# The layout of the gate matrices in scratch: by token block, or by groups of four i1

## The chip, the cores and the metric

The kernel runs on one core of a Trainium2 chip. The metric is the device time of one execution in microseconds (us): from the start of the program on the core to its end, as a median over runs. A profiled execution is one more, recorded by the hardware profiler; its span runs from the first to the last instruction.

A core has TensorE (PE, matrix products; its weight loads are listed as PEld), VectorE (DVE), ScalarE (ACT), GpSimd (POOL) and SyncE (SP). Sixteen DMA engines move data between HBM and on-chip memory, in packets. Here SyncE issues all plain transfers, in the order of the program, into one queue (q1 in the profile), and GpSimd issues the indirect gathers into another (q0).

## What is computed

The reference is one layer of a decoder trunk for 1024 prompt tokens and 8 sample tokens: three branches (a dilated window attention, a convolution, an attention into memory) that are gated, summed and projected onto x, and then a mixer of very many single-neuron experts. Only the mixer matters here:

```python
def peer(x, w_pq, sub_keys, u_tab, v_tab):
    ...
        e = (jnp.take_along_axis(i1, ci // PEER_TOPK, axis=-1) * N_KEYS
             + jnp.take_along_axis(i2, ci % PEER_TOPK, axis=-1))
        g = jax.nn.softmax(sc, axis=-1)
    ...
        a = jnp.einsum('bd,bed->be', xb, u_tab[e], preferred_element_type=jnp.float32)
        hg = g * jax.nn.gelu(a)
        out = jnp.einsum('be,bed->bd', hg, v_tab[e].astype(jnp.float32))
```

There are 128 x 128 experts, numbered by a pair (i1, i2). Each token picks 128 of them (8 heads, 16 each), with a gate weight for each.

## The kernel before

The tokens are split. For the last three blocks of 128 prompt tokens, and for the samples, `peer_gather` fetches the picked rows of u and v one slot at a time: one indirect DMA on GpSimd's queue brings 128 rows of 8 KB (tile `uv`), VectorE makes the dot product (L985), ScalarE the gelu (L990), VectorE adds into `gacc` (L995). For the first five blocks (640 tokens) `peer_dense` computes every expert and multiplies by a gate that is zero for the experts not picked.

Those gates are built in `gate_build`, 32 tokens at a time (TC = 32): TensorE multiplies one-hot matrices (L1061, L1062), and ScalarE copies the result into `stg` (L1063), which holds i2 in its 128 partitions and, in each partition, i1 by 32 tokens, 16 KB in all. One DMA stores it to the scratch tensor `gscr` in HBM (L1066). There are 640 / 32 = 20 such stores of 2 MB. `stg` has two buffers. The first 16 stores are issued while the second half of the front (projections, gates, attention units) runs, the last four while the last top-k and the start of the dense part run.

`peer_dense` walks over the 128 values of i1 in groups of six (C = 6). For each i1 it loads the rows of u (`ur`, L1097), splits them into a high and a low part, makes the products with 640 tokens (`pa`), the gelu (L1107, tile `ge`) and the product with the gates (L1109). The gates come from tiles `Gt` with two buffers, each for four values of i1 (GC = 4) and loaded by one DMA (L1094): 32 loads of 1.25 MB. After the six i1 of a group come, for each half of the columns, six loads of v (`vr`, three buffers, L1121), their split (`vh` on ScalarE, L158; `vl` on VectorE, L159), the products `pv` into five banks of PSUM, and the sums into `dacc` on VectorE (L1129).

The order of the instructions on every engine, and of the DMAs that SyncE issues, is fixed when the program is built: a scheduler places them by the priorities in the code. The gather's instructions are placed between those of the dense part on VectorE, ScalarE and GpSimd, and no engine leaves its order at run time. A DMA waits, on SyncE, until the buffer that it writes is free, and all later DMAs wait with it.

Of the kernel before, what the change touches and what calls it, by code (L numbers as in the profile page):

```python
# [9 lines left out]
F32 = mybir.dt.float32  # L10
# [11 lines left out]
P = 128  # L22
# [7 lines left out]
NA = NAB * P  # L30
# [4 lines left out]
BIG = 3e38  # L35
GSCALE = 16384.0
TC = 32
LNPOS = (16, 12)
MIDPOS = (24, 20)
LATEPOS = (24, 22)  # L40
# [6 lines left out]
def peer_trunk(tc, I, O):  # L47
    nc = tc.nc
# [10 lines left out]
    with contextlib.ExitStack() as es:  # L59
        const = es.enter_context(tc.tile_pool(name="const", bufs=1))  # L60
        dram = es.enter_context(tc.tile_pool(name="dram", bufs=1, space=DRAM))
# [74 lines left out]
        oscr = [dram.tile([SEQ, 520], F32, name=f"oscr{g}") for g in range(3)]  # L136
        x1scr = dram.tile([NTOK, D], F32, name="x1scr")
        h2scr = dram.tile([NTOK, D], F32, name="h2scr")
        gscr = dram.tile([NA // TC, P, P, TC], F32, name="gscr")
        mscr = dram.tile([SEQ, 512], F32, name="mscr")  # L140
        gtscr = dram.tile([24, P, HALF + NS], F32, name="gtscr")
        saccd = dram.tile([P, D], F32, name="saccd")
# [14 lines left out]
        def split_load(raw, hi, lo):  # L157
            nc.scalar.copy(hi, raw)  # L158
            nc.vector.tensor_tensor(lo, raw, hi.bitcast(F32), op=OP.subtract)  # L159
# [98 lines left out]
        def front(hf, keep, wp):  # L258
# [53 lines left out]
            with tc.tile_pool(name=f"mix{hf}", bufs=1) as mx, banks(f"mix{hf}"):  # L312
# [337 lines left out]
                order = [*range(8, 24), *range(8)]  # L650
                for q in range(LNPOS[hf]):
                    gate(order[q])
# [12 lines left out]
                bh, bl = conv_norm()  # L665
                for q in range(LNPOS[hf], MIDPOS[hf]):
                    gate(order[q])
# [348 lines left out]
        def gate_build(gb, pgs, toks, TB, prio0=None, prio_step=0):  # L1016

            step = 0
            for t0 in range(toks[0], toks[1], TC):
                bi = t0 // P  # L1020
                if t0 % P == 0:
                    pt = pgs.tile([P, 4, P], F32, tag="pG", bufs=2, name=f"igT{bi}")
                    for q in range(3):
                        nc.tensor.transpose(pt[:, q], igT[bi][:, q], ident)
                    nc.scalar.copy(igT[bi], pt[:, 0:3])
                    ig = gb.tile([P, 4, P, 2], F16, tag="ig", bufs=1, name=f"ig{bi}")

                    def twice(q):
                        return igT[bi][:, q].unsqueeze(2).to_broadcast([P, P, 2])

                    for q in range(2):
                        nc.vector.tensor_copy(ig[:, q], twice(q))
                    nc.vector.tensor_scalar(ig[:, 2], twice(2), GSCALE, None, op0=OP.mult)
                    nc.vector.scalar_tensor_tensor(
                        ig[:, 3], twice(2), GSCALE, ig[:, 2], op0=OP.mult, op1=OP.subtract
                    )
                stg = gb.tile([P, P, TC], F32, tag="stg", bufs=2, name=f"stg{t0}")
                for tb in range(0, TC, TB):
                    ts_ = slice(t0 % P + tb, t0 % P + tb + TB)
                    if prio0 is not None:  # L1040
                        tc.cur_priority = prio0 + step * prio_step
                        step += TB // 4
                    o1, o2, wh = (
                        gb.tile([P, TB, P // 2, 2], F16, tag=f"oh{q}", bufs=2, name=f"oh{q}_{t0}_{tb}") for q in range(3)
                    )
                    shape = [P, TB, P // 2, 2]
                    ioB = iotaT.rearrange("p (a e) -> p a e", e=2).unsqueeze(1).to_broadcast(shape)

                    def cols(q):
                        return ig[:, q, ts_].unsqueeze(2).to_broadcast(shape)  # L1050

                    nc.vector.tensor_tensor(o1, ioB, cols(0), op=OP.is_equal)
                    nc.vector.tensor_tensor(o2, ioB, cols(1), op=OP.is_equal)
                    nc.vector.tensor_tensor(wh, o1, cols(2), op=OP.mult)
                    wl = o1
                    nc.vector.tensor_tensor(wl, o1, cols(3), op=OP.mult)
                    for t4 in range(0, TB, 4):
                        pG = pgs.tile([P, 4, P], F32, tag="pG", bufs=2, name=f"pG{t0}_{tb + t4}")
                        for t in range(t4, t4 + 4):
                            a, h, l = (x[:, t].rearrange("p a e -> p (a e)") for x in (o2, wh, wl))  # L1060
                            nc.tensor.matmul(pG[:, t - t4], a, h, start=True, stop=False)  # L1061
                            nc.tensor.matmul(pG[:, t - t4], a, l, start=False, stop=True)  # L1062
                        nc.scalar.activation(  # L1063
                            stg[:, :, tb + t4 : tb + t4 + 4], pG.rearrange("p t i -> p i t"), AF.Copy, scale=1.0 / GSCALE
                        )
                nc.sync.dma_start(gscr[t0 // TC], stg)  # L1066

        def peer_dense():
            NB = NAB
            with (  # L1070
# [10 lines left out]
                for b in range(NB):  # L1081
                    nc.sync.dma_start(acc[:, b], x1scr[b * P : (b + 1) * P, :])
                C = 6
                GC = 4
                HN = NA // 2
                for c in range(-(-P // C)):
                    if c == 5:
                        sample_out(dq)
                    hgs = []
                    group = range(c * C, min(P, c * C + C))  # L1090
                    for i1 in group:
                        if i1 % GC == 0:
                            Gt = dq.tile([P, NA // TC, GC, TC], F32, tag="Gt", bufs=2, name=f"Gt{i1}")
                            nc.sync.dma_start(Gt, gscr[:, :, i1 : i1 + GC, :].rearrange("n p i t -> p n i t"))  # L1094
                        raw = dp.tile([P, KD * P], F32, tag="uraw", bufs=2, name=f"ur{i1}")
                        uh = dp.tile([P, KD * P], F32R, tag="uh", bufs=2, name=f"uh{i1}")
                        nc.sync.dma_start(raw, I["uT"][i1])  # L1097
                        ul = dp.tile([P, KD * P], F32R, tag="ul", bufs=2, name=f"ul{i1}")
                        split_load(raw, uh, ul)
                        ge = dh.tile([P, NA], F32, tag="ge", bufs=2, name=f"ge{i1}")  # L1100
                        for q in range(2):
                            cs = slice(q * HN, (q + 1) * HN)
                            pa = t_tile(f"pa{i1}{q}")
                            for k in range(KD):
                                ks = slice(k * P, (k + 1) * P)
                                mm3(pa[:, :HN], uh[:, ks], ul[:, ks], h2h[:, k, cs], h2l[:, k, cs], k == 0, k == KD - 1)
                            nc.scalar.activation(ge[:, cs], pa[:, :HN], AF.Gelu_apprx_tanh)  # L1107
                        g3 = ge.rearrange("p (n t) -> p n t", t=TC)
                        nc.vector.tensor_tensor(g3, g3, Gt[:, :, i1 % GC, :], op=OP.mult)  # L1109
                        hh = dh.tile([P, NA], F32R, tag="hh", bufs=C, name=f"hh{i1}")  # L1110
                        hl = dh.tile([P, NA], F32R, tag="hl", bufs=C, name=f"hl{i1}")
                        nc.scalar.copy(hh, ge)
                        nc.vector.tensor_tensor(hl, ge, hh.bitcast(F32), op=OP.subtract)
                        hgs.append((hh, hl))
                    for q in range(2):
                        qs = slice(q * 512, q * 512 + 512)
                        pv = [mm_tile(f"pv{c}{q}{tb}") for tb in range(NB)]
                        for j, i1 in enumerate(group):
                            raw = dq.tile([P, 512], F32, tag="vraw", bufs=3, name=f"vr{i1}{q}")
                            vh = dq.tile([P, 512], F32R, tag="vh", bufs=3, name=f"vh{i1}{q}")  # L1120
                            nc.sync.dma_start(raw, I["v_tab"][i1 * P : (i1 + 1) * P, qs])  # L1121
                            vl = dq.tile([P, 512], F32R, tag="vl", bufs=3, name=f"vl{i1}{q}")
                            split_load(raw, vh, vl)
                            hh, hl = hgs[j]
                            for tb in range(NB):
                                ts_ = slice(tb * P, (tb + 1) * P)
                                mm3(pv[tb], hh[:, ts_], hl[:, ts_], vh, vl, j == 0, j == len(group) - 1)
                        for tb in range(NB):
                            nc.vector.tensor_tensor(acc[:, tb, qs], acc[:, tb, qs], pv[tb], op=OP.add)  # L1129
                            if group[-1] == P - 1:  # L1130
                                nc.sync.dma_start(O["y"][tb * P : (tb + 1) * P, qs], acc[:, tb, qs])
# [35 lines left out]
        tc.cur_priority = base  # L1167
        phase["mm"] = 5
        peer_dense()


# [79 lines left out]
```

## Time and profile before

| | us |
|---|---|
| median of 3 runs | 3676.84 |
| lowest and highest of the 3 | 3676.28, 3680.1 |
| the profiled execution | 3687.05 |
| its span, first to last instruction | 3685.3 |

The profile was taken on one execution, and durations below are its own. Busy time of an engine is time in which it works on an instruction; a wait is idle time of an engine together with what ended it. The clock of TensorE is granted in steps: 1.0 is full speed, 0.5 half. The view of DMA packets counts the packets that began in a stretch, by queue, with the share of 16 engines' time that they took; a packet is one run of bytes, and very small ones carry the signals that a transfer has landed. The span starts at 0 us in all views.

### The profile page before, as it was taken

How to read it: one execution, taken by the hardware profiler on the slowest of the kernel's cores; microseconds unless marked ns; L12 is line 12 of the kernel's file. 1: busy time of each engine (PE TensorE's matmuls, PEld its weight loads, DVE VectorE, ACT ScalarE, POOL GpSimd, SP SyncE). 2: the span in 40 equal slices, each digit the busy share in tenths (PEclk: the TensorE clock that was granted, in tenths of full speed). 3: DMA queues.
4: the chain of work that ended last, by engine and by line, in shares of the span. 5: the costliest groups of instructions: out<-in, count | busy, mean ns of one | idle time of the engine just before them, and what ended most of it. 6: DMA issues, size and time to landing. Idle time of an engine off the chain costs nothing.

```text
span 3685.3 us, 55180 instructions
## 1 busy us (share of the span) xinstructions
PE 3371.1 (91%) x19969; PEld 2953.3 (80%) x19969; DVE 2904.0 (79%) x6280; ACT 1492.0 (40%) x3519; POOL 565.3 (15%) x398
## 2 busy tenths in 40 slices
PE   8987999898888899787699999899998989899999
PEld 6766988697666778577699888899897979798988
DVE  4358554499999668789988888789887878797987
ACT  5553552235765465344433333333332323233332
POOL 0000000000000000100023333223333322233321
PEclk9997999999999999898799999999999999999999
DMA  5468456423355557744588888899887989798886
GB/s 179 137 191 266 148 181 185 150 93 109 109 191 184 182 184 262 261 157 153 195 298 325 322 326 315 306 333 338 318 332 288 334 293 334 286 329 315 323 321 236
DMA packets 338454, 902.08 MB, mean 245 GB/s; under 512 B 32588, under 2 KB 140276, under 8 KB 285436
## 3 DMA queue, kind: packets, MB, share of 16 engines
q1 hardware_dynamic: 281732, 487.49, 39.7%
q0 software_dynamic: 56448, 411.07, 29.3%
q8 instruction: 156, 2.56, 0.3%
q14 instruction: 118, 0.97, 0.1%
HBM read 804.09 MB, written 94.83 MB: 244 GB/s over the span
## 4 chain that ended last, share of the span: by engine, by line
PE 29%; issue 28%; DVE 16%; DMA 15%; POOL 9%; ACT 3%; SPq 1%; POOLq 0%; DVEq 0%; ACTq 0%
POOL uv L981 9%; DMA uv<-in_uv,idxB 5%; PE pg L175 2%; PE pg L174 2%; PE pg L176 2%; DMA vr<-in_v_tab 1%; PE pv L174 1%; PE pv L175 1%; PE pv L176 1%; DMA wko<-kscr 1%; PE pa L176 1%; PE pa L174 1%; PE pa L175 1%; PE p_q L175 1%; DVE gacc L995 1%
## 5 line engine op out<-in xcount | busy, mean ns | idle before, releaser
L981 POOL DMA_INDIRECT uv<-in_uv,idxB x384 | 554.1, 1443 | 1548.3 <-DVE gacc L995 1209.6
L174 PE MATMUL pa<-h2Ah,uh 128*128 128x320 f32 x2048 | 636.6, 311 | 9.9 <-ACT ge L1107 6.5
L176 PE MATMUL pa<-h2Ah,ul 128*128 128x320 f32 x2048 | 634.2, 311 | 2.8 <-DVE ul L159 2.8
L175 PE MATMUL pa<-h2Al,uh 128*128 128x320 f32 x2048 | 635.6, 310 | 0.0
L985 DVE CUSTOM_DVE_ANT_0 uv<-uv,gh 128x1024 f32<-128x1024 f32 x392 | 477.7, 1221 | 124.8 <-DMA uv<-in_uv,idxB 115.6
L174 PE MATMUL pv<-vh,hh 128*128 128x512 f32 x1280 | 478.6, 398 | 65.1 <-ACT vh L158 34.8
L995 DVE SCALAR_TENSOR_TENSOR gacc<-uv,av,gacc 128x1024 f32<-128x1024 f32 x392 | 502.1, 1281 | 16.5 <-ACT av L993 11.7
L175 PE MATMUL pv<-vl,hh 128*128 128x512 f32 x1280 | 505.9, 395 | 2.3 <-DVE vl L159 2.3
L176 PE MATMUL pv<-vh,hl 128*128 128x512 f32 x1280 | 500.7, 394 | 0.0
L174 PEld LDWEIGHTS pa<-h2Ah,uh 128*128 128x128 f32 x2048 | 388.1, 189 | 15.7 <-ACT ge L1107 6.9
L176 PEld LDWEIGHTS pa<-h2Ah,ul 128*128 128x128 f32 x2048 | 387.2, 189 | 6.4 <-DVE ul L159 3.5
L175 PEld LDWEIGHTS pa<-h2Al,uh 128*128 128x128 f32 x2048 | 387.7, 189 | 2.9
L158 ACT CAST vh<-vr 128x512 fp32r<-128x512 f32 x256 | 158.1, 619 | 459.0 <-PE pv L176 231.5
L174 PEld LDWEIGHTS pv<-vh,hh 128*128 128x128 f32 x1280 | 244.4, 192 | 116.5 <-ACT vh L158 64.4
L175 PEld LDWEIGHTS pv<-vl,hh 128*128 128x128 f32 x1280 | 244.0, 191 | 52.3 <-DVE vl L159 4.3
L176 PEld LDWEIGHTS pv<-vh,hl 128*128 128x128 f32 x1280 | 244.0, 191 | 50.7
L159 DVE TENSOR_TENSOR vl<-vr,vh 128x512 fp32r<-128x512 f32 x256 | 175.3, 687 | 102.0 <-ACT vh L158 100.2
L981 POOL DMA_INDIRECT uv<-in_uv,idxS x8 | 10.5, 1314 | 1532.6 <-DMA th<-gtscr 1484.6
L158 ACT CAST uh<-ur 128x1024 fp32r<-128x1024 f32 x128 | 134.2, 1049 | 182.0 <-PE pa L175 139.1
L174 PE MATMUL pg<-hTh,wh_g 128*128 128x260 f32 (+1 forms) x576 | 195.7, 340 | 0.6 <-ACT tg L647 0.6
L175 PE MATMUL pg<-hTl,wh_g 128*128 128x260 f32 (+1 forms) x576 | 194.3, 337 | 0.0
L176 PE MATMUL pg<-hTh,wl_g 128*128 128x260 f32 (+1 forms) x576 | 193.5, 336 | 0.0
(559 smaller groups left out, 7363.4 us busy)
## 6 DMA issues: line engine op xcount, KB each, us to landing
ur<-in_uT SPq DMA_DIRECT2D x128, 512.0 KB
vr<-in_v_tab SPq DMA_DIRECT2D x256, 256.0 KB
gscr<-stg SPq DMA_DIRECT2D x20, 2048.0 KB
Gt<-gscr SPq DMA_DIRECT2D x32, 1280.0 KB
wr_g<-in_w_col SPq DMA_DIRECT2D x48, 512.0 KB
wr_q<-in_w_in SPq DMA_DIRECT2D x24, 512.0 KB
wr_u<-in_w_col SPq DMA_DIRECT2D x16, 512.0 KB
wr_pq<-in_w_col SPq DMA_DIRECT2D x16, 512.0 KB
```

The source lines that it names most:

```text
L158: nc.scalar.copy(hi, raw)
L159: nc.vector.tensor_tensor(lo, raw, hi.bitcast(F32), op=OP.subtract)
L174: nc.tensor.matmul(out, ah, bh, start=start, stop=False)
L175: nc.tensor.matmul(out, ah, bl, start=False, stop=False)
L176: nc.tensor.matmul(out, al, bh, start=False, stop=stop)
L981: nc.gpsimd.indirect_dma_start(out=uv, out_offset=None, in_=I["uv"], in_offset=bass.IndirectOffsetOnAxis(ap=col, axis=0),)
L985: nc.vector.tensor_tensor_reduce(out=uv[:, 0:D], in0=uv[:, 0:D], in1=h2, scale=1.0, scalar=0.0, op0=OP.mult, op1=OP.add, accum_out=av[:, s ...
L995: nc.vector.scalar_tensor_tensor(acc, uv[:, D:], av[:, j : j + 1], acc, op0=OP.mult, op1=OP.add)
```

## The change

`gscr` gets another order of axes. Before, it is token block (20), i2 (128), i1 (128), token in block (32). After, it is group of four i1 (32), i2 (128), token block (20), i1 in group (4), token in block (32). The store of one token block and the load of one group follow: a load now reads one unbroken run in each partition, and a store writes 32 runs in each. The tiles in on-chip memory, the number of DMAs and the bytes stay as they are.

```diff
+GC = 4
...
-        gscr = dram.tile([NA // TC, P, P, TC], F32, name="gscr")
+        gscr = dram.tile([P // GC, P, NA // TC, GC, TC], F32, name="gscr")
...
-                nc.sync.dma_start(gscr[t0 // TC], stg)
+                nc.sync.dma_start(
+                    gscr[:, :, t0 // TC].rearrange("c p i t -> p c i t"), stg.rearrange("p (c i) t -> p c i t", i=GC)
+                )
...
-                GC = 4
...
-                            nc.sync.dma_start(Gt, gscr[:, :, i1 : i1 + GC, :].rearrange("n p i t -> p n i t"))
+                            nc.sync.dma_start(Gt, gscr[i1 // GC])
```

## Rows read from the trace of the kernel before

**Rows 1.** The page, its first part: busy us (share of span) xinstructions.
```profile
PE 3371.1 (91%) x19969; PEld 2953.3 (80%) x19969; DVE 2904.0 (79%) x6280; ACT 1492.0 (40%) x3519; POOL 565.3 (15%) x398
```

**Rows 2.** Instructions on gscr: issue ns min/median/max, first and last start.
```profile
L1094 SPq DMA_DIRECT2D Gt<-gscr x32: 377/377/3931, 1814.5 to 3527.6; - x32
L1066 SPq DMA_DIRECT2D gscr<-stg x20: 319/323/429, 1052.2 to 1807.3; - x20
```

**Rows 3.** Busy time by stretch; columns in the first line.
```profile
core 0: us, PE busy (x) PEld busy (x) DVE busy (x) ACT busy (x) POOL busy (x), PEclk, DMA share, GB/s
...
1340.00:1480.00 140.00, 137.27 (x914) 114.28 (x913) 107.56 (x247) 77.54 (x182) 0.00 (x0) 1.00 0.69 240
...
1814.00:3681.00 1867.00, 1794.54 (x9916) 1630.01 (x9916) 1567.40 (x2108) 600.84 (x1346) 550.39 (x380) 0.98 0.86 312
2330.00:2650.00 320.00, 320.00 (x1805) 292.62 (x1804) 276.93 (x358) 107.83 (x244) 101.16 (x71) 1.00 0.90 331
3019.00:3025.00 6.00, 5.89 (x16) 4.76 (x17) 6.00 (x11) 0.68 (x3) 0.00 (x0) 0.52 0.24 73
```

**Rows 4.** From 1814 us: a group of matmuls (idle after bar); a ScalarE wait.
```profile
L174 PE MATMUL pv<-vh,hh 128*128 128x512 f32 x1280 | 478.6, 398 | 65.1 <-ACT vh L158 34.8 <-DVE dacc L1129 30.2
...
ACT vh L158 <- DMA vr<-in_v_tab: 226.3, 52, 14.3
```

**Rows 5.** Timeline, one stall, then first and last: start, us, what, [idle before].
```profile
2992.38 0.38 SPq L1094 DMA_DIRECT2D Gt<-gscr  x1
2994.27 10.38 SPq L1121 DMA_DIRECT2D vr<-in_v_tab  x2
...
3017.02 1.28 ACT L158 CAST vh<-vr 128x512 fp32r<-128x512 f32 x2 [14.33 <-DMA vr<-in_v_tab]
...
3019.11 0.76 PE L174 MATMUL pv<-vh,hh 128*128 128x512 f32 x1 [11.17 <-ACT vh L158]
...
2132.26 0.79 PE L174 MATMUL pv<-vh,hh 128*128 128x512 f32 x1 [5.10 <-ACT vh L158]
...
3548.55 0.80 PE L174 MATMUL pv<-vh,hh 128*128 128x512 f32 x1 [4.52 <-ACT vh L158]
```

**Rows 6.** DMA packets begun from 3005 to 3007 us: packets, MB, share of 16 engines.
```profile
q0 software_dynamic: 101, 0.77, 93.8%
q1 hardware_dynamic: 107, 0.05, 9.7%
```

**Rows 7.** The same from 1845.5 to 1849, 1363 to 1367, 413.9 to 414.7 us.
```profile
q1 hardware_dynamic: 2027, 1.04, 105.3%
...
q1 hardware_dynamic: 109, 1.79, 107.7%
...
DMA packets 148, 0.14 MB, mean 172 GB/s; under 512 B 19, under 2 KB 147, under 8 KB 148
...
q1 hardware_dynamic: 148, 0.14, 49.8%
```

**Rows 8.** The gather: VectorE's waits from 1814 us; the last issue.
```profile
DVE uv L985 <- DMA uv<-in_uv,idxB: 115.6, 93, 5.0
...
3645.46 1.45 POOL L981 DMA_INDIRECT uv<-in_uv,idxB  x1 [0.30 <-issue]
```

**Rows 9.** TensorE's waits, 1050 to 1480 us: us in total, times, longest.
```profile
PE wT L380 <- DMA wkp<-kscr: 15.3, 7, 3.7
PE wT L380 <- DMA wko<-kscr: 9.4, 4, 3.8
...
PE wo L332 <- DMA wvo<-vscr: 3.7, 3, 2.1
```

**Rows 10.** Timeline: a store, and waits of TensorE behind it.
```profile
1208.71 0.34 SPq L1066 DMA_DIRECT2D gscr<-stg  x1
...
1224.27 0.33 PE L380 MATMUL wT<-ident,wkp 128*128 128x128 f32 x1 [1.59 <-DMA wkp<-kscr]
1228.38 0.47 PE L380 MATMUL wT<-ident,wko 128*128 128x128 f32 x1 [3.78 <-DMA wko<-kscr]
```

**Rows 11.** TensorE's waits from 1730 to 1820 us.
```profile
PE pa L174 <- ACT ge L1107: 6.5, 1, 6.5
...
PE tr_A L190 <- DMA hx<-h2scr: 1.7, 2, 1.3
```

## The prediction

> **What bounds the kernel now.** I read the page first, for where the engines are busy, then one table of stretches, then the waits of TensorE in the last stretch, then one of those waits instruction by instruction, and last the packets of the DMA queues around it. TensorE works 3371.1 of 3685.3 us [rows 1], so what can be won lies in the 314 us in which it does nothing, and in the time that its clock is low.
>
> The two halves of the change sit in different stages. The 20 stores to scratch are issued between 1052.2 and 1807.3 us, the 32 dense loads between 1814.5 and 3527.6 us [rows 2]. I call the two stages the front and the dense stage. In the dense stage TensorE is busy 1794.54 of 1867 us at a clock of 0.98; from 2330 to 2650 us it is busy all 320 us at clock 1.00, with the gather beside it (71 spans on GpSimd) and the DMA engines 90% busy [rows 3]. So nothing steady limits that stage below TensorE's own pace; what it loses, it loses in single stalls. One line has nearly all of them: the first matmul on a new tile of v waited 65.1 us, 34.8 for the cast of v and 30.2 for the sums into dacc [rows 4]. The cast itself waited 226.3 us for the load of v [rows 4].
>
> One such stall in order [rows 5]: at 2992.38 us SyncE issues a Gt load, at 2994.27 two loads of v, the second of which is held up (10.38 us for the two). ScalarE's cast of v starts only at 3017.02, after 14.33 us of waiting for v, and TensorE goes on at 3019.11 after 11.17 us of nothing. The sums into dacc stand behind v's remainder in VectorE's order, so the 30.2 us are mostly the same lateness by another name. Seven stalls of more than 4 us have this shape, each 20 to 27 us after a Gt issue; the first and the last are in the group (5.10 and 4.52 us), and together they are 57.6 of the 65.1. They come about every 180 us, which is two groups of six i1: a Gt tile serves four i1, so three Gt loads fall on two groups, and one of the three is issued just when the next loads of v are needed. Behind the other two Gt loads TensorE has work, as 2330 to 2650 us shows.
>
> Why the Gt load is slow there is in the queues. Between 3005 and 3007 us the gather's queue moved 101 packets and took 93.8% of the engines, SyncE's queue moved 107 and took 9.7% [rows 6]. The two queues take turns packet by packet: a gather packet is 8 KB, a Gt packet 512 B. A Gt load is 2560 such packets, 160 for each of 16 engines, and crawls until the gathers in flight are through; v stands behind it in the same queue.
>
> **The change, part by part.** Counts follow from the code: a Gt tile is 20 x 4 x 32 floats in each partition, so a load goes from 20 runs of 512 B in each partition to one of 10 KB, and a store from one run of 16 KB to 32 of 512 B. 32 x 2560 and 20 x 4096 are both 81920: the number of short packets stays, and they move from the dense stage to the front.
>
> Prices. With nothing beside it, the Gt load moved 2027 packets in 3.5 us at 105.3% of 16 engines: 1.053 x 16 x 3500 / 2027 = 29.1 ns each. The store's 16 KB packets: 1.077 x 16 x 4000 / 109 = 632 ns each [rows 7]. A 10 KB packet lies between a gather's 8 KB (0.938 x 16 x 2000 / 101 = 297 ns, [rows 6]) and 632; by bytes I take 395. So a load needs 160 x 29.1 = 4.7 us of each engine now and 8 x 0.395 = 3.2 us after, 1.5 us less. A store needs 8 x 0.632 = 5.1 us now. The trace has no dense run of 512 B stores; the nearest row is that of gtscr stores with runs of 1040 B: 0.498 x 16 x 800 = 6370 ns for 148 packets, 19 of them tiny, so near 48 ns for a run of 1040 B [rows 7]. The bounds are the bytes alone (632 / 32 = 20 ns, no loss) and a price by the packet whatever its size (48 ns). Half a 1040 B run is 24 ns, and I take the load's 29.1, which has the same size: 256 x 29.1 = 7.5 us, 2.4 us more a store. Engine time alone is thus a wash (32 x 1.5 = 48 us less, 20 x 2.4 = 48 us more); what counts is who waits.
>
> The Trainium skill says in "DMA: Bandwidth & Descriptors", section "Latency and other measured facts", that HBM copies at a row pitch of 2 or 4 MiB fell from 207 to 164 and 103 GB/s. The new store's chunks lie 1.25 MiB apart. The old load's chunks lay 2 MiB apart and still took 29.1 ns, which speaks against such a loss for reads; no row shows it for stores. By that rule's worst figure a store packet would take twice 29.1 ns, and with that price in the sum below the time would be an estimate of 3735 us.
>
> Dense stage, gain. In turns with gather packets, 8 Gt packets are through after 8 turns, 8 x (395 + 297) = 5.5 us at most, where they now take until the gathers run dry: between the issue and the cast lie 24.6 us. The loads of v behind it come about 10 us earlier, and the seven stalls of 57.6 us shrink to some 4 (those of 9 to 11 us keep 0 to 1): 54 us. After a stall the clock is down: from 3019 to 3025 us TensorE worked at 0.52 [rows 3], near the lower of its two levels (1.2 against 2.4 GHz), which costs 2.9 us; seven times less some remainder is 16 us. Against it: a gather that shares its turns with 8 packets of 395 ns lands up to 3.2 us later, where VectorE already waits 115.6 us in 93 waits for gathers [rows 8]. That hurts where TensorE hangs on VectorE, in one Gt load of three: ten times 0 to 3.2 us; I take 8 us in all. Dense stage: 54 + 16 - 8 = 62 us less. The next wait behind these is the gather itself: its last issue is at 3645.46 us [rows 8], some 35 us ahead of the end of TensorE's work, and it is tied to the dense work by VectorE's fixed order, so it moves with it.
>
> Front, cost. No gather runs beside the stores, so loads simply stand 2.4 us longer behind them in SyncE's queue. SyncE also holds its next issue while a long list of packets goes out (3931 ns at most behind a Gt load [rows 2]), with 4096 packets longer; what is held would stand behind the store anyway, so I add nothing. From 1050 to 1480 us TensorE waited 15.3 us for wkp, 9.4 for wko and 3.7 for wvo, 14 waits [rows 9]. They follow eight of the sixteen stores there: the store of 1208.71 us, for one, is followed by the waits at 1224.27 and 1228.38 us [rows 10]. Eight times 2.4 is 19 us. The other eight, six of them after 1340 us, where TensorE idles 2.7 of 140 us [rows 3], are covered by gate matmuls; if that cover were thin, they would cost up to 2.4 us each, 19 us more. The four stores after 1730 us: two hx loads that TensorE already waits for (1.7 us in 2 waits, [rows 11]) come 2.4 us later each, 5 us; the last store delays the first Gt by 2.4, and that Gt itself is 1.5 shorter, 1 us on the stall of 6.5 us [rows 11]. Clock after these longer waits: 2 us. Front: 19 + 5 + 1 + 2 = 27 us more.
>
> At no cost: ScalarE's copy into stg, since its two buffers are filled 20 to 35 us apart and a store reads one for 7.5; the Gt buffers, asked for a whole i1 quartet (some 58 us) ahead; GpSimd's own queue, past which nothing is moved.
>
> Sum: -62 + 27 = -35 us on the profiled execution, 3687.05 to 3652 us. That execution is 0.28% above the median of the three runs, so on the median 3676.84 - 35 = 3642 us.
>
> **Rivals.** (1) The front hides the stores: the waits there end on something else, of the 27 us only 5 remain, and the dense gain is whole (70). For it: the sixteen stores already leave half without a wait. Against: wkp and wko are on the chain of waits right behind a store. Time: 3676.84 - 65 = 3612 us.
>
> (2) The stall changes hands: gathers lose turns to 10 KB packets, VectorE waits for uv instead of v, and TensorE keeps its gaps, 20 us won in place of 62. Against it, the total packet time falls and 2330 to 2650 us runs full at 90% DMA. Time: 3676.84 - 20 + 27 = 3684 us. A change without effect looks much the same.
>
> (3) Slower: the scattered stores write at well over 29 ns a packet. The place is the eight stores followed by waits, plus the last three. To eat 62 us they must each grow by 5.6 us, (5.1 + 5.6) / 256 = 42 ns a packet. At 48 ns each grows by 256 x 48 - 5060 = 7.2 us; 11 x 7.2 = 79, and some 12 us from stores that are now covered: 3676.84 - 62 + 91 = 3706 us. Against it stands the same 1040 B row, read by its bytes.
>
> **How the numbers follow.** Forecast 62%, rival 1 15%, rival 2 12%, rival 3 11%. The forecast's own range: dense gain 45 to 75, front 15 to 45, so 3610 to 3675. The range given takes in rivals 1 and 2, 3600 to 3690, and leaves out rival 3. What a measurement of this kernel can tell from no change is about 0.2%, 7.4 us, so faster means under 3669.5. Faster: 0.62 x 0.95 + 0.15 = 0.74. Same: 0.03 of the forecast and two thirds of rival 2, 0.11. Slower: rival 3 and the rest of rival 2, 0.15.
>
> **What would show it.** In the dense stage, packets of 10 KB of about 395 ns, the waits of vh and dacc at the first v matmul near 10 us in place of 65.1, and VectorE's wait for uv grown by no more than some 30 us. In the front, packets of 512 B near 29 ns, a store near 7.5 us, waits for wkp, wko and wvo near 50 us in place of 28.4. The prediction is wrong if a 512 B store packet takes over 42 ns, if the stalls of v stay with the short Gt load, or if the covered stores turn out not to be covered.

## The result

The changed kernel takes 3622.15 us (median of 4 runs, 3616.64 to 3624.78); the kernel before took 3678.47 beside it (3676.28 to 3685.16). The ratio is 0.9849, 95% interval 0.9827 to 0.9871: some 56 us less, between 47 and 64. The prediction said 35 less, 3642, with a range of 3600 to 3690. The profiled execution went from 3687.05 to 3621.67 us, its span from 3685.3 to 3619.6. Every engine runs its instructions in the same order as before, but for two pairs of neighbours on VectorE far ahead of the gates, so the two traces can be laid side by side. The profiled execution before lies 9 us above its median and the one after at its median, so the stages below differ by 65.7 us together, not by the 56 of the medians.

The issues of the two DMAs on `gscr`, after (issue ns min/median/max, first and last start in us), answer to [rows 2]:

```profile
L1096 SPq DMA_DIRECT2D Gt<-gscr x32: 326/326/1108, 1841.6 to 3466.3; - x32
L1067 SPq DMA_DIRECT2D gscr<-stg x20: 370/371/1243, 1048.5 to 1832.3; - x20
```

The first Gt load is issued at 1841.6 us, where it was 1814.5. The front has become 27.1 us longer; from the first store to the first Gt load, which leaves out 3.7 us by which this execution was ahead, it is 762.3 before and 793.1 after. The dense stage, from the first Gt issue to the end of TensorE's work, was 1866.7 us and is 1773.9, 92.8 less. Both stages by busy time, before and then after (first the sixteen stores of the front, then the dense stage):

```profile
core 0: us, PE busy (x) PEld busy (x) DVE busy (x) ACT busy (x) POOL busy (x), PEclk, DMA share, GB/s
1052.20:1456.50 404.30, 361.06 (x2454) 292.32 (x2453) 320.10 (x613) 218.63 (x500) 0.00 (x0) 0.96 0.58 199
1814.50:3681.20 1866.70, 1794.73 (x9916) 1630.01 (x9916) 1566.90 (x2103) 600.84 (x1346) 550.39 (x380) 0.98 0.86 312
```

```profile
core 0: us, PE busy (x) PEld busy (x) DVE busy (x) ACT busy (x) POOL busy (x), PEclk, DMA share, GB/s
1048.50:1473.00 424.50, 372.03 (x2463) 301.38 (x2462) 320.50 (x614) 219.17 (x500) 0.00 (x0) 0.92 0.63 190
1841.60:3615.50 1773.90, 1769.10 (x9916) 1613.41 (x9916) 1564.46 (x2081) 601.91 (x1346) 563.70 (x380) 1.00 0.87 329
```

In the dense stage TensorE's idle time went from 72.0 us (1866.70 - 1794.73) to 4.8, and its busy time, for the same 9916 matmuls, from 1794.73 to 1769.10, at a clock of 1.00 in place of 0.98. The two parts, 67.2 and 25.6, are the whole 92.8 us. Beyond these 4.8 us nothing is left to win there but TensorE's own pace.

One stall of [rows 5] looks like this after; SyncE, then ScalarE:

```profile
2969.74 0.33 SPq L1096 DMA_DIRECT2D Gt<-gscr  x1
2972.96 4.01 SPq L1123 DMA_DIRECT2D vr<-in_v_tab  x2
...
2984.18 0.62 ACT L159 CAST vh<-vr 128x512 fp32r<-128x512 f32 x1 [2.24 <-DMA vr<-in_v_tab]
```

The cast of v starts 14.4 us after the Gt issue; it was 24.6. TensorE's wait after it is gone: the first matmul on a new v tile, in the whole dense stage, waited 0.9 us in place of 65.1 [rows 4], and VectorE's waits for gathers became shorter, not longer (115.6 in [rows 8]):

```profile
L175 PE MATMUL pv<-vh,hh 128*128 128x512 f32 x1280 | 468.5, 390 | 0.9 <-ACT vh L159 0.9
...
DVE uv L986 <- DMA uv<-in_uv,idxB: 97.8, 68, 4.8
```

The packets, from 1377 to 1382 us (one store alone) and from 2445 to 2449 (a Gt load beside gathers), in the columns of [rows 6]:

```profile
q1 hardware_dynamic: 2833, 1.45, 99.9%
...
q1 hardware_dynamic: 152, 1.30, 76.6%
q0 software_dynamic: 51, 0.42, 24.6%
```

A 512 B store packet takes 0.999 x 16 x 5000 / 2833 = 28.2 ns. In the other stretch the queue of the Gt load gets 76.6% of the engines, where [rows 6] gave it 9.7%. Most of its 152 packets are the 10 KB ones: 1.30 MB are some 127 of them, and 0.766 x 16 x 4000 / 127 = 386 ns. This load is one that TensorE's work covers; at the stall above, from 2974 to 2979 us, the share was 62.2%, with loads of v already behind it.

The costs in the front: TensorE's waits from 1050 to 1480 us, then two from 1750 to 1846 (us in total, times, longest), to be laid beside [rows 9, 11].

```profile
PE wT L381 <- DMA wkp<-kscr: 18.5, 6, 5.0
PE wo L333 <- DMA wvo<-vscr: 9.4, 4, 4.3
PE wT L381 <- DMA wko<-kscr: 8.4, 3, 3.1
...
PE pa L175 <- ACT ge L1109: 8.6, 1, 8.6
...
PE tr_A L191 <- DMA hx<-h2scr: 5.5, 2, 3.2
```

The three waits for keys and values are 36.3 us together, 28.4 before. That is 8 us, less than the 20 by which the stretch of sixteen stores grew; the rest is in the table above, where TensorE's clock there fell from 0.96 to 0.92 and its busy time rose by 11 us.

### The profile page after: what moved, and what is told of

Read it like the earlier page. It is cut to its first block, busy times and chain, and to the rows that moved or that the text cites. A ratio compares the mean times of both kernels' runs of the same rounds, so it can differ in the third digit from the quotient of the medians.

```text
span 3619.6 us, 55180 instructions
## 1 busy us (share of the span) xinstructions
PE 3351.8 (93%) x19969; PEld 2943.1 (81%) x19969; DVE 2905.5 (80%) x6280; ACT 1494.1 (41%) x3519; POOL 579.8 (16%) x398
## 4 chain that ended last, share of the span: by engine, by line
PE 71%; DVE 13%; DMA 9%; issue 3%; ACT 3%; POOL 1%; SPq 1%; DVEq 0%; ACTq 0%; POOLq 0%
PE pa L175 8%; PE pa L177 8%; PE pa L176 8%; PE pv L175 8%; PE pv L176 8%; PE pv L177 8%; PE pg L176 2%; PE pg L175 2%; PE pg L177 2%; PE p_q L176 1%; PE p_q L177 1%; DMA wko<-kscr 1%; PE p_q L175 1%; DMA th<-gtscr 1%; DVE y L576 1%
## 5 line engine op out<-in xcount | busy, mean ns | idle before, releaser
L982 POOL DMA_INDIRECT uv<-in_uv,idxB x384 | 567.5, 1478 | 1450.6 <-DVE gacc L996 1109.6
L175 PE MATMUL pv<-vh,hh 128*128 128x512 f32 x1280 | 468.5, 390 | 0.9 <-ACT vh L159 0.9
```

Of the source, the lines that this page charges most:

```text
L175: nc.tensor.matmul(out, ah, bh, start=start, stop=False)
L982: nc.gpsimd.indirect_dma_start(out=uv, out_offset=None, in_=I["uv"], in_offset=bass.IndirectOffsetOnAxis(ap=col, axis=0),)
```

## The experiments

Times are medians. The kernel before was run again beside the others: 3678.37 us beside e1, e2, e3 and e5, 3678.1 beside e4, e6 and e9, 3682.2 beside e10; the ratios are against these. "Dense" is the stage from the first Gt issue to the end of TensorE's work, "front" the time from the first store's issue to the first Gt issue, both from one profiled execution. Single executions differ: that of the kernel before lies 9 us above its median, that of e6 11 us below, and the front with the old stores is 762.3 before but 766.5 to 767.9 in e1, e3, e4 and e10. Differences of some 5 us between two lines say nothing.

| kernel | us | ratio (95%) | front | dense |
|---|---|---|---|---|
| before | 3678 | | 762.3 | 1866.7 |
| changed | 3622.15 | 0.9849 (0.9827 to 0.9871) | 793.1 | 1773.9 |
| e1 loads alone | 3601.36 | 0.9798 (0.9754 to 0.9842) | 766.6 | 1774.2 |
| e2 stores alone | 3699.84 | 1.0061 (1.0036 to 1.0086) | 785.0 | 1861.6 |
| e3 loads in 2 KB runs | 3614.43 | 0.9828 (0.9784 to 0.9872) | 767.0 | 1798.3 |
| e4 loads on ScalarE's queue | 3603.78 | 0.9803 (0.977 to 0.9836) | 767.9 | 1782.8 |
| e5 stores on ScalarE's queue | 3619.98 | 0.9848 (0.9804 to 0.9892) | 775.1 | 1790.2 |
| e6 stores on GpSimd's queue | 3631.52 | 0.9879 (0.9846 to 0.9912) | 797.0 | 1772.3 |
| e9 stores in 1 KB runs | 3654.62 | 0.9933 (0.991 to 0.9957) | 777.9 | 1820.0 |
| e10 load's runs 1 KB apart | 3654.3 | 0.9925 (0.9896 to 0.9955) | 766.5 | 1833.8 |

In e1, e2, e3, e9 and e10 the instructions stand in the order of the kernel before but for one pair of neighbours at most; the runs of those DMAs alone differ. In e4 several hundred have changed places between 1821 and 2170 us, and the order is that of the kernel before from there on; in e5 and e6 many instructions have.

### e1 and e2: each half alone

```diff
# e1, against the kernel before
+ flat = gscr.rearrange("n p i t -> (n p i t)").rearrange("(g p n i t) -> g p n i t", p=P, n=NA // TC, i=GC, t=TC)
- nc.sync.dma_start(Gt, gscr[:, :, i1 : i1 + GC, :].rearrange("n p i t -> p n i t"))
+ nc.sync.dma_start(Gt, flat[P // GC - 1 - i1 // GC])
# e2, against the changed kernel
+ flat = gscr.rearrange("c p n i t -> (c p n i t)").rearrange("(n p i t) -> n p i t", p=P, i=P, t=TC)
- nc.sync.dma_start(Gt, gscr[i1 // GC])
+ nc.sync.dma_start(Gt, flat[:, :, i1 : i1 + GC, :].rearrange("n p i t -> p n i t"))
```

> Only the loads are changed: the stores stay one run of 16 KB per partition in the old layout, and a Gt load reads one unbroken run of 10 KB per partition from that scratch (in the reverse order of groups, so that the first load still waits for the last store). The gates that it reads are therefore not the right ones; the work is the same. Theory (turns: a load of 8 packets per engine gets through between gather packets, one of 160 does not): the dense stage, counted from the first Gt issue to the end of TensorE's work, falls by the same 93 us as in the changed kernel and the front stays: 3678 - 93 = 3585, between 3570 and 3600. Rival (only engine time counts): 32 loads x 1.5 us = 48 us, so 3630.

> Only the stores are changed: 32 runs of 512 B per partition in the new layout; the loads keep 20 runs of 512 B at 2 MiB steps. The gates that are read are not the right ones. Theory: the front gets 27 us longer (eight stores with waits behind them, 2.4 us each, and the end), the dense stage keeps its stalls: 3678 + 27 = 3705, between 3693 and 3720. Rival (the 27 us between the two profiles are jitter of the front, or come from elsewhere): within 7 us of 3678.

The loads alone win 77 us of the median, and their dense stage (1774.2) is that of the changed kernel; the stores alone cost 21 (13 to 32 by the interval), and their dense stage keeps its stalls. 21 - 77 = -56, which is what the change measured: the halves add up. Both came out on the side of the theory, e1 some 1 us beyond the slow edge of it, e2 inside. The matmul on a new v tile in e2, from 1842 us, in the columns of [rows 4]:

```profile
L175 PE MATMUL pv<-vh,hh 128*128 128x512 f32 x1280 | 477.9, 398 | 56.9 <-DVE dacc L1132 31.4 <-ACT vh L159 25.5
```

### e3: fewer turns, or less engine time?

```diff
# against the kernel before
+ flat = gscr.rearrange("n p i t -> (n p i t)").rearrange("(n p x) -> n p x", n=5, p=P)
+ g512 = slice(i1 // GC * 512, i1 // GC * 512 + 512)
- nc.sync.dma_start(Gt, gscr[:, :, i1 : i1 + GC, :].rearrange("n p i t -> p n i t"))
+ nc.sync.dma_start(
+     Gt.rearrange("p n i t -> p (n i t)").rearrange("p (n x) -> p n x", n=5),
+     flat[:, :, g512].rearrange("n p x -> p n x"),
+ )
```

> As the kernel before, but a Gt load has 5 runs of 2 KB per partition in place of 20 of 512 B (from the old layout, so the gates read are not the right ones). Own time of a load: 40 packets x 84 ns = 3.4 us of each engine, close to the 3.1 us of 8 packets of 10 KB, but 40 turns against the 32 packets of four gathers in flight. Theory (turns): the load still has to wait until the gathers in flight are through, most stalls of v stay, gain 0 to 35 us: 3643 to 3678. Rival (own time of the load counts): 1.3 of the 1.6 us are won, so some 80% of 93 us: 3604.

My theory missed here: 64 us won, and the dense stage 68 shorter, 74% of the 92.8. The rival's number is close, but e4 below speaks against its reason. What I had wrong is the step from the Gt load to the stall. A load of 40 packets still takes turns, but TensorE has work in hand: in [rows 5] v was 24.6 us behind the Gt issue and TensorE idled 11.17, so some 13.4 us are covered. In e3 the same place of the program (SyncE, ScalarE), and then the matmul on a new v tile from 1842 us, read:

```profile
2959.96 0.38 SPq L1096 DMA_DIRECT2D Gt<-gscr  x1
2963.83 4.01 SPq L1126 DMA_DIRECT2D vr<-in_v_tab  x2
...
2973.47 0.62 ACT L158 CAST vh<-vr 128x512 fp32r<-128x512 f32 x1 [2.90 <-DMA vr<-in_v_tab]
...
L174 PE MATMUL pv<-vh,hh 128*128 128x512 f32 x1278 | 469.9, 392 | 11.6 <-DVE dacc L1134 10.0 <-ACT vh L158 1.1 <-ACT av L993 0.5
```

The cast comes 13.5 us after the issue, at the edge of what is covered, and TensorE does not wait here; of the 11.6 us, 9.4 are two other stalls that stayed. How much is covered differs from place to place: the changed kernel's cast came 14.4 us after the issue without a wait, that of e1 16.5 with a wait of 1.4. So the gain looks more like a threshold than a proportion: once v is early enough, nothing more is won. No run set out to test that.

### e4: the same short packets, in a queue of their own

```diff
# against the kernel before
- nc.sync.dma_start(Gt, gscr[:, :, i1 : i1 + GC, :].rearrange("n p i t -> p n i t"))
+ nc.scalar.dma_start(Gt, gscr[:, :, i1 : i1 + GC, :].rearrange("n p i t -> p n i t"))
```

> The kernel before (old layout, Gt loads in 512 B runs), with the 32 Gt loads issued by ScalarE on its own hardware queue. Theory (v is late because it stands behind Gt in SyncE's queue): v takes turns with Gt and the gathers and lands early although Gt has as many packets and as much engine time as before; the dense stage loses most of its 72 us of stalls: gain 60 to 93, so 3585 to 3618. Rival (the engine time of the 512 B packets, or the gathers' backlog, is what makes v late, in whichever queue): dense stage as before, 3670 to 3680. Third possibility: ScalarE's casts stand behind an issue of Gt that waits for its buffer: stalls of ScalarE in their place, slower than 3678.

This settles the dense stage. The packets are the old ones, 512 B and 2 MiB apart, and they need the same engine time: on the page of e4 their queue is a row of its own, 82432 packets in 4.3% of 16 engines' time, 0.043 x 3600.2 = 155 us, or 4.8 us a load, where [rows 7] gave 4.7. Still the dense stage falls to 1782.8 us. The DMA queues on that page; the packets from 2955 to 2960 us, while a Gt load, loads of v and gathers are all in flight; and ScalarE, which issues the Gt load itself, beside SyncE, with the matmul on a new v tile from 1842 us:

```profile
q1 hardware_dynamic: 199300, 445.54, 36.4%
q0 software_dynamic: 56448, 411.07, 29.8%
q10 hardware_dynamic: 82432, 41.95, 4.3%
```

```profile
q0 software_dynamic: 147, 1.06, 50.8%
q1 hardware_dynamic: 218, 0.52, 27.5%
q10 hardware_dynamic: 663, 0.34, 23.6%
```

```profile
2951.67 0.37 ACTq L1094 DMA_DIRECT2D Gt<-gscr  x1
...
2954.77 7.55 SPq L1121 DMA_DIRECT2D vr<-in_v_tab  x3
...
2962.02 0.60 ACT L158 CAST vh<-vr 128x512 fp32r<-128x512 f32 x1
...
L174 PE MATMUL pv<-vh,hh 128*128 128x512 f32 x1276 | 467.1, 391 | 4.0 <-DVE dacc L1129 3.8 <-ACT vh L158 0.2
```

Three queues share the engines, v is cast 10.4 us after the Gt issue without a wait for its load, and TensorE's wait at a new v tile is 4.0 us from 1842 us on. The Gt load itself came no sooner: between 2970 and 2977 us, 18 to 25 us after its issue, 87 packets of its queue still went out. It was the place behind Gt in one queue that cost, not the packets' own time. Nor was it the other order: from the ninth Gt issue on, where the order is the old one, the rest of the stage takes 1413 us, where the kernel before took 1493 and the changed one 1410. The front is as long as in the other runs with the old stores (767.9; 766.5 to 767.0 in e1, e3 and e10), and all runs of e4 (3603.12 to 3606.03) lie below all of the changed kernel's (3616.64 to 3624.78), with the old layout. Only e1 is as fast, and it doesn't read the right gates. The Trainium skill ("DMA: Bandwidth & Descriptors", section "Issuing engines are not separate DMA queues") says that issuing from several engines only saves the time of the issue. Here it was worth 74 us, and the measurement decides. The first load of v was issued 3.1 us behind Gt, even later than the 1.9 of [rows 5]; what changed is when it came through.

### e5 and e6: the scattered stores in another queue

```diff
# e5, against the changed kernel
- nc.sync.dma_start(gscr[:, :, t0 // TC].rearrange("c p i t -> p c i t"), ...)
+ nc.scalar.dma_start(gscr[:, :, t0 // TC].rearrange("c p i t -> p c i t"), ...)
# e6: nc.gpsimd.dma_start(...)
```

> The changed kernel, with the 20 stores issued by ScalarE on its own hardware queue in place of SyncE. Theory (what the stores cost is that loads stand behind them in one queue): loads of 2 KB packets now take turns with 512 B packets, the 27 us go and part of the 28 us of waits for wkp, wko and wvo that the kernel before has: 3622 - 27 to 3622 - 45, so 3577 to 3595. Rival (the engines' time for the stores is what costs, in whichever queue): 3622, or a little more for the issues on ScalarE.

> The changed kernel, with the 20 stores issued by GpSimd on the gather's queue; GpSimd has nothing else to do in most of the front. The scheduler places many instructions in another order than in the changed kernel. Theory (stores cost because loads stand behind them): from the first store to the sixteenth 405 us as in the kernel before, not 424 as in the changed one; total 3590 to 3605 if the dense stage is as in the changed kernel. Rival (engine time of the stores): 424 us there, total 3622 or more.

Both missed: e5's total is the rival's, e6's is above its rival's 3622. And both are muddied by the other order of the instructions. In e5 the stretch of sixteen stores is back at 408.6 us (404.3 before, 424.5 after), as the theory says, but its dense stage is 16 us longer than that of the changed kernel, which ate the gain. In e6 the stretch stays at 428.9 us, the rival's 424 or more. Its trace shows one possible reason: on GpSimd's queue the store does not go out in 512 B packets. From 1249 to 1255 us, in the midst of a store:

```profile
q0 software_dynamic: 379, 1.54, 84.2%
q1 hardware_dynamic: 177, 0.35, 15.7%
```

A packet there has 4 KB and takes 0.842 x 16 x 6000 / 379 = 213 ns, so a load's packet that takes turns with the store has that much to wait each time. TensorE's waits for wkp, 18.5 us in the changed kernel, are 42.1 here. How much of this is the packets and how much the new order stays open, and with it whether the stores cost by what stands behind them.

### e9 and e10: the length of a store, and where a load's runs lie

```diff
# e9, against the changed kernel
- gscr = dram.tile([P // GC, P, NA // TC, GC, TC], F32, name="gscr")
+ gscr = dram.tile([P // 8, P, NA // TC, 8, TC], F32, name="gscr")
...
- stg.rearrange("p (c i) t -> p c i t", i=GC)
+ stg.rearrange("p (c i) t -> p c i t", i=8)
...
- nc.sync.dma_start(Gt, gscr[i1 // GC])
+ nc.sync.dma_start(Gt, gscr[i1 // 8][:, :, i1 % 8 : i1 % 8 + GC, :])
# e10, against the kernel before
+ flat = gscr.rearrange("n p i t -> (n p i t)").rearrange("(g p n i t) -> g p n i t", p=P, n=NA // TC, i=2 * GC, t=TC)
- nc.sync.dma_start(Gt, gscr[:, :, i1 : i1 + GC, :].rearrange("n p i t -> p n i t"))
+ nc.sync.dma_start(Gt, flat[P // (2 * GC) - 1 - i1 // (2 * GC)][:, :, i1 % (2 * GC) : i1 % (2 * GC) + GC, :])
```

> Scratch by groups of eight i1: a store is 16 runs of 1 KB per partition, a Gt load 20 runs of 512 B as in the kernel before. A store takes 128 packets of 47 ns, 6.0 us, 1.0 us more than in the kernel before, where the 512 B runs take 2.4 more. Theory (the front's cost goes with the length of the store): 27 x 1.0 / 2.4 = 11 us, total 3689, and from the first store to the first Gt issue some 773 us (762 to 767 with the old stores, 785 to 793 with 512 B runs). Rival (any scattered store costs the whole): 3700, 785 us or more. The dense stage keeps its stalls.

> The kernel before, stores and order unchanged, but a Gt load's 20 runs of 512 B lie 1 KB apart in scratch in place of 2 MiB apart (from the old layout, so the gates read are not the right ones); it stands for the load of the run with 1 KB stores without those stores. That run's dense stage was 1820 us in place of 1867, although its Gt packets were as many and took as long. Theory A (where the runs lie: near ones get through sooner beside the gathers): dense stage near 1820, total near 3640, 3625 to 3655. Theory B (the dense stage of that run came out shorter since its longer front set gathers and Gt loads in another phase to each other): dense stage near 1860, total within 12 of 3678.

In e9 the front is 777.9 us, 15.6 longer than before and 10 to 11 longer than in e1, e3, e4 and e10, where 11 was expected, and short of the 785.0 and 793.1 of the 512 B stores. So the stores' cost grows with their length, as far as single executions tell: the two with the same 512 B stores are 8 us apart. The total was off by 34 us for a reason that I had not seen: the dense stage came out at 1820.0 us although the Gt load has its old 2560 packets. e10 keeps the old stores and order, has those runs 1 KB apart alone, and shows the same: 28 us less than before (17 to 38), dense 1833.8. So where the runs lie counts, theory A, at the slow edge of its span; with the distance of the runs, the step from partition to partition also went from 16 to 20 KB. The waits at a new v tile from 1842 us, e9 and then e10:

```profile
L175 PE MATMUL pv<-vh,hh 128*128 128x512 f32 x1280 | 473.6, 394 | 31.0 <-DVE dacc L1131 16.3 <-ACT vh L159 14.6
```

```profile
L174 PE MATMUL pv<-vh,hh 128*128 128x512 f32 x1278 | 475.8, 396 | 39.8 <-DVE dacc L1130 28.7 <-ACT vh L158 9.0 <-ACT hh L1113 2.0
```

Why near runs get through sooner was not found: what fills the time between the packets beside the gathers, the runs don't tell.

## Why the prediction was right, point by point

**What bounds it.** Right. The stalls behind Gt loads were what the dense stage lost; with them gone TensorE's idle time there is 4.8 us. e1 (loads alone) and e4 (loads elsewhere) show it from two sides.

**The mechanism of the stall.** Right in that v stood behind Gt and Gt took turns with gathers; e4 shows the first directly. The trace of the kernel before has a sign for the second that I read past. I took 2330 to 2650 us for Gt loads that TensorE's work covers, but it also holds one with v right behind it (Gt issued at 2469.36 us, v at 2472.73). From 2470 to 2477 us the gather's queue started no packet, SyncE's had 90.8% of the engines, and TensorE did not wait. Nor do the stalls come every 180 us throughout: between 2320 and 2838 us none is over 4 us. Not seen: that the loads' runs lying 2 MiB apart added to it (e10), and that TensorE's work in hand, some 13 us and more, makes the gain much like a threshold (e3).

**Prices.** The store packet, 29.1 ns taken, took 28.2; the 10 KB packet, 395 taken, some 386. The 1040 B row was the right neighbour. Of the 101 packets of [rows 6], 7 are signals, so a gather packet took 319 ns, not 297; little hung on it. The Trainium skill's rule on row pitch ("DMA: Bandwidth & Descriptors", section "Latency and other measured facts") is on the distance from partition to partition, 10 KB here; it did not show itself in the stores' chunks, 1.25 MiB apart, whose 28.2 ns is no more than the loads' 29.1.

**Dense stage.** The term was too small: 62 forecast, 92.8 measured between the two profiled executions, 77 by the medians (e1 against the kernel before; e2 against the changed kernel gives 78). Three pieces, by the profiles: all idle time but 4.8 us went, 67 where I had 54, since the waits below 4 us went as well and almost nothing stayed of the seven stalls; the time of low clock behind them gave 25.6 where I had 16; and the 8 us that gathers were to cost did not come, VectorE's waits for them fell by 18 us. The last piece is the error of kind: I let the gather lose turns to long packets. Why the waits fell is open. That VectorE, no longer stuck behind v, asks for the next gather sooner does not fit the other runs: with v on time in e4 they are 119.4 us, and with some of the stalls left in e9 79.8.

**Front.** 27 forecast; 27.1 by the first Gt issue, 30.8 from the first store, 21 by e2's median. The sum lies inside e2's interval (13 to 32), but its make-up was wrong, so that it came out is partly luck: the waits for keys and values grew by 8 us where I had 19, while the low clock cost more than the 2 us that I gave it (busy time up by 11 in the stretch of sixteen stores, at a clock of 0.92 in place of 0.96). The hx waits grew by 3.8 (5 forecast), the first Gt's by 2.1 (1 forecast). That no gather runs beside the stores was not quite so for the last four: from 1759 to 1765 us, in the midst of one in the kernel before, 26 packets of the gather's queue went out.

**Rivals.** The front did not hide the stores (e2 falls outside no change by its interval), the stall did not change hands, and the stores did not write slowly. That e1 is 21 us faster than the changed kernel shows what the second half of the change costs. The forecast's own range was added up wrongly: its bounds give 3617 to 3677, not 3610 to 3675; the measured 3622 lies in both.

## What to carry to other kernels

Look at what stands behind a transfer in its queue before looking at the transfer: a load that nobody waits for can cost 70 us by the one issued after it. Where one queue carries 8 KB gather packets and the other short runs, the short runs can get as little as a tenth of the engines (9.7% in [rows 6]), and what stands behind them is late. Lengthen the runs, or give them a queue of their own, and try the second first, since it needs no other layout and here won more (74 us against 56). A price moved from one stage to another is not a wash: what counts is how much work each stage has in hand when the transfer is late.

## What the runs showed of the hardware

- Where both queues had work, their packets went out in nearly equal numbers, not bytes: 101 of the gather to 107 of 512 B in [rows 6], and 231 to 197, most of them 2 KB of v, from 3010 to 3015 us. Other stretches are less even (51 to 152 in the changed kernel). A run of 512 B is a packet of its own when SyncE or ScalarE issues it (82432 packets for 41.95 MB in e4), while on GpSimd's queue eight such runs went as one packet of 4 KB (213 ns, e6).
- With runs of 512 B read 1 KB apart (e10) the dense stage was 33 us shorter than with those 2 MiB apart (1833.8 against 1866.7; 28 by the medians), with as many packets.
- A third queue beside the two others took its share: 50.8, 27.5 and 23.6% in e4's stretch, and v no longer waited for the Gt load to go out.
